# Hybrid decoder trunk: the squares of the features begin 24 bytes into wider tiles and come first in GpSimd's sums of squares; an unread tile of ones is dropped

## The chip, the cores and the metric

One core of a Trainium2 chip runs the whole program in one launch. The metric is the device time of one execution in microseconds (us). The kernel before took 1767.26 us in the median of three runs (1767.1 to 1767.7).

## What is computed

The reference is a decoder trunk of two layers on a float32 input of 512 tokens by 1024 features. Each layer is two half-step feed-forward networks (FFNs) around a mixer, and each of the three begins with an RMS norm of x over its features:

```
def rms_norm(x, g):
    y = xf * lax.rsqrt(jnp.mean(xf * xf, axis=-1, keepdims=True) + EPS)
    return (y * g)

x = x + 0.5 * swiglu(rms_norm(x, ffn1_norm[l]), ...)     # 1024 -> 2816 -> 1024
h = rms_norm(x, mix_norm[l])                              # [a | g | q | k | v] = h @ w_in[l]
x = x + concatenate([conv_out, diff_out]) @ w_out[l]      # causal depthwise conv; differential attention
x = x + 0.5 * swiglu(rms_norm(x, ffn2_norm[l]), ...)
```

The change concerns the sum of `xf * xf` over the features, which the norm needs.

## The kernel before, in words

**Layout.** x lies transposed in SBUF: a tile of 128 partitions (features within a block) by 8 blocks k by 512 tokens, called `x[:, k, :]`. A matrix product is made of float32r products of high and low parts: `hi` is a rounded copy, `lo` the rest, and each block needs three matmuls (hi·hi, hi·lo, lo·hi). Weights arrive by DMA in `wraw` tiles and are split into `whi` (ScalarE, L106 and L370) and `wlo` (VectorE or GpSimd, L107; VectorE, L374).

**The norm's preparation.** Class `Prep` makes, for the next sub-layer, from each block k of x as soon as the previous sub-layer has finished it:
- `acth`: the block times its gain, rounded (ScalarE, L231);
- `actl`: the rest (VectorE, L232, with x and `acth` as tensors from SBUF);
- the squares: ScalarE squares the block into `sq`, a ring of two buffers, or for k = 0 directly into `ssum` (L240), and GpSimd adds `sq` to the running sum `ssum` (L244). The very first sub-layer does these seven sums on VectorE instead.

The first products of the next sub-layer use `acth` and `actl` without the norm's factor. Beside them TensorE transposes `ssum` (L201, `rows_rstd`), VectorE sums over features (L205), and the factor, one number for each token, is spread back (L214, `spread`) and multiplied in behind the products. So the sums of squares are needed by L201, some matmuls after the last block of x is finished. There are five such stages with seven sums on GpSimd each: the end of the first FFN and of the mixer in each layer, and the end of the second FFN of the first layer.

**Other users.** The FFN reuses the two `sq` buffers, and that of `ssum`, for parts `hs` of its hidden features (`Gated.part`), which are moving operands of matmuls at L387. The mixer uses `sq` for squares of queries, keys and outputs (L912, L1067), and the setup for a few small tiles. The mixer's convolution has sums of squares of its own, in a form that matters here (L961 to L963):

```
sq = mt.tile([P, SEQ + 8], F32, tag="csq", name="csq", bufs=1)[:, GAP : GAP + SEQ]
S.activation(sq, y, AF.Square)
G.tensor_tensor(csum, sq, csum, op=ALU.add)
```

`GAP` is 6 elements, 24 bytes. The convolution's taps are summed by GpSimd as well (L982: `yp` begins `GAP` elements into a tile of `SEQ + 8`, and `prod` at a tile's start). So are the sums of weight blocks for the FFN's products (`Unit.sums`, L360 to L363): `g1` and `g2` lie in a tile that begins `GAP` elements in; `u1` and `u2` are, in the units of the down projection, blocks of one tile from its start.

**Addresses.** Tiles of a pool get consecutive places in each partition, in the order in which their tags are first used. The tile `ones` lies in the first pool, behind `ident`, and nothing reads it; in its pool and in those behind it, every tile starts on a multiple of 32 bytes. `ssum` and the two `sq` buffers are neighbours, 2048 bytes each.

**Order.** Each engine runs its instructions in one queue; the order between independent steps is chosen when the program is built, and is fixed then.

Of the kernel before, what the change touches and what calls it, by code (L numbers as in the profile page):

```python
# [11 lines left out]
F32 = mybir.dt.float32  # L12
# [3 lines left out]
ALU = mybir.AluOpType  # L16
AX = mybir.AxisListType

P = 128
DEPTH = 2  # L20
SEQ = 512
# [28 lines left out]
GAP = 6  # L50
# [20 lines left out]
def trunk(ctx: ExitStack, tc: tile.TileContext, xt, par, lamv, relb, onehot,  # L71
          gu1, dn1, wag, wqkv, wout, gu2, dn2, out):
    nc = tc.nc
    V, S, G, T = nc.vector, nc.scalar, nc.gpsimd, nc.tensor

    const = ctx.enter_context(tc.tile_pool(name="const", bufs=1))
# [4 lines left out]
    tmp = ctx.enter_context(tc.tile_pool(name="tmp", bufs=2))  # L81
# [97 lines left out]
    lead = [[tuple(t[1:]) for t in lead[2 * m : 2 * m + 2]] for m in range(2)]  # L179
    ident = const.tile([P, P], F32, tag="ident", name="ident")  # L180
    make_identity(nc, ident)
    ones = const.tile([P, P], F32, tag="ones", name="ones")
    G.memset(ones, 1.0)
    mhalf = const.tile([P, 16], F32, tag="mhalf", name="mhalf")
    G.memset(mhalf, -0.5)

# [34 lines left out]
    class Prep:  # L221
# [14 lines left out]
                self.squares(k)  # L236

        def squares(self, k, pin=False):
            sq = self.s if k == 0 else tmp.tile([P, SEQ], F32, tag="sq", name="sq")
            square = S.activation(sq, x[:, k, :], AF.Square)  # L240
            if pin:
                tc.keep_in_program_order(square)
            if k > 0:
                (V if pin else G).tensor_tensor(self.s, self.s, sq, op=ALU.add)  # L244

        def __getitem__(self, k):
            return self.hi[:, k, :], self.lo[:, k, :]
# [1009 lines left out]
```

## Time and profile before

| | us |
|---|---|
| median of three runs | 1767.26 (1767.1 to 1767.7) |
| the profiled execution | 1767.6 |
| its span, first to last instruction | 1765.8 |
| TensorE busy (PE) | 1756.3 (99%) |
| VectorE busy (DVE) | 1394.2 (79%) |
| ScalarE busy (ACT) | 989.1 (56%) |
| GpSimd busy (POOL) | 869.5 (49%) |
| all sums of squares on GpSimd, L244, 35 of 128x512 | 52.2 |

The granted TensorE clock was 1.000 throughout. PE is matmuls, PEld the weight loads that overlap them. In rows by line and form, what follows the first bar is busy time in us and the mean ns of one instruction, and what follows the second is the idle time of the engine just before these instructions, with what ended it. In rows of one tile or line, three numbers are the shortest, middle and longest duration in ns. In rows of the waits, the numbers are us in total, how often, and the longest. In rows in order of time: start, length in us, engine, line, operation, out<-in. A matmul's end is modelled: the starts of matmuls tell more than their lengths.

### The profile page before, as it was taken

Reading aid. Unit: us, or ns where it says so; the run is one execution under the profiler, and the core shown is the slowest. Engines: PE = TensorE matmul, PEld = TensorE weight load, DVE = VectorE, ACT = ScalarE, POOL = GpSimd, SP = SyncE. Lnnn points to the kernel's source line nnn. Section 1 sums busy time; section 2 is a strip of 40 time slices with the busy share of each in tenths; the row PEclk is TensorE's granted clock in tenths of the full one; section 3 lists DMA queues with packets and bytes.
Section 4 is the critical chain, followed back from the end, with each engine's and each line's share of the span. In section 5 each row is a group of like instructions: output and inputs, shape, how many; then the busy total and the mean of one; then the engine's idle time right before and its main releaser. Section 6 shows DMA issues by size and latency. Waiting matters only on the chain.

```text
span 1765.8 us, 30565 instructions
## 1 busy us (share of the span) xinstructions
PE 1756.3 (99%) x11869; PEld 1620.8 (92%) x11869; DVE 1394.2 (79%) x2021; ACT 989.1 (56%) x1591; POOL 869.5 (49%) x665
## 2 busy tenths in 40 slices
PE   9999999999999999999999999999999999999999
PEld 7899999988788899999988999999887888999998
DVE  6978878868857868878778788777788588788785
ACT  6456565545845456556534665565558354565653
POOL 3165655369753146555303565543687432556551
PEclk9999999999999999999999999999999999999999
DMA  6233333333122233333332333334230232333332
GB/s 226 92 117 100 106 108 105 127 104 99 33 84 84 84 96 108 109 102 117 106 108 72 108 99 105 108 98 154 72 119 25 72 108 72 107 98 108 108 106 75
DMA packets 82930, 177.89 MB, mean 101 GB/s; under 512 B 8951, under 2 KB 30726, under 8 KB 82784
## 3 DMA queue, kind: packets, MB, share of 16 engines
q1 hardware_dynamic: 81184, 174.10, 31.2%
q8 instruction: 93, 1.52, 0.4%
q0 software_dynamic: 1312, 1.67, 0.3%
q14 instruction: 53, 0.43, 0.1%
q10 hardware_dynamic: 288, 0.16, 0.0%
HBM read 173.79 MB, written 3.42 MB: 100 GB/s over the span
## 4 chain that ended last, share of the span: by engine, by line
PE 97%; DVE 2%; DMA 0%; issue 0%; SPq 0%; ACT 0%; DVEq 0%
PE ps_pair L387 57%; PE ps_pair L147 5%; PE ps_pair L146 5%; PE ps_pair L143 5%; PE ps_d L147 2%; PE ps_d L146 2%; PE ps_d L143 2%; PE ps_sc L1028 2%; PE ps_d L387 2%; PE ps_pair L904 2%; PE ps_pair L905 2%; PE ps_pair L906 2%; PE ps_out L146 1%; PE ps_out L147 1%; PE ps_out L143 1%; PE ps_o L1058 1%
## 5 line engine op out<-in xcount | busy, mean ns | idle before, releaser
L374 DVE TENSOR_TENSOR wlo<-wraw,whi 128x1024 fp32r<-128x1024 f32 (+2 forms) x400 | 505.6, 1264 | 167.3 <-ACT whi L370 166.6
L370 ACT ACTIVATE whi<-wraw 128x1024 fp32r<-128x1024 f32 (+2 forms) x400 | 379.2, 949 | 329.4 <-PE ps_pair L387 184.5
L360 POOL TENSOR_TENSOR wraw<-wraw 128x512 f32<-128x512 f32 (+1 forms) x100 | 113.1, 1131 | 605.9 <-DVE wlo L374 393.9
L387 PE MATMUL ps_pair<-acth,wlo 128*128 128x256 f32 x1088 | 307.9, 283 | 0.0
L387 PE MATMUL ps_pair<-actl,whi 128*128 128x256 f32 x1088 | 307.9, 283 | 0.0
L387 PE MATMUL ps_pair<-acth,whi 128*128 128x256 f32 x1088 | 307.9, 283 | 0.0
L387 PE MATMUL ps_pair<-th,whi 128*128 128x256 f32 x816 | 230.9, 283 | 0.0
L387 PE MATMUL ps_pair<-tl,whi 128*128 128x256 f32 x816 | 230.9, 283 | 0.0
L387 PE MATMUL ps_pair<-th,wlo 128*128 128x256 f32 x816 | 230.9, 283 | 0.0
L387 PEld LDWEIGHTS ps_pair<-actl,whi 128*128 128x128 f32 x1088 | 208.9, 192 | 0.2
L387 PEld LDWEIGHTS ps_pair<-acth,whi 128*128 128x128 f32 x1088 | 208.9, 192 | 0.2
L106 ACT ACTIVATE whi<-wraw 128x1024 fp32r<-128x1024 f32 (+3 forms) x124 | 123.2, 1002 | 153.0 <-PE ps_pair L146 85.7
L387 PEld LDWEIGHTS ps_pair<-acth,wlo 128*128 128x128 f32 x1088 | 208.9, 192 | 0.0
L362 POOL TENSOR_TENSOR wraw<-wraw 128x512 f32<-128x512 f32 (+1 forms) x100 | 176.5, 1765 | 7.8
L146 PE MATMUL ps_pair<-actl,whi 128*128 128x512 f32 x448 | 174.7, 391 | 0.3
L143 PE MATMUL ps_pair<-acth,whi 128*128 128x512 f32 x448 | 173.7, 392 | 0.7 <-ACT whi L106 0.6
L147 PE MATMUL ps_pair<-acth,wlo 128*128 128x512 f32 x448 | 173.8, 390 | 0.0
L387 PEld LDWEIGHTS ps_pair<-th,whi 128*128 128x128 f32 x816 | 156.7, 192 | 0.0
L387 PEld LDWEIGHTS ps_pair<-tl,whi 128*128 128x128 f32 x816 | 156.7, 192 | 0.0
L387 PEld LDWEIGHTS ps_pair<-th,wlo 128*128 128x128 f32 x816 | 156.7, 192 | 0.0
L363 POOL TENSOR_TENSOR wraw<-wraw 128x512 f32<-128x512 f32 (+1 forms) x100 | 143.1, 1431 | 7.8
L387 PE MATMUL ps_pair<-hl,whi 128*128 128x256 f32 (+1 forms) x496 | 145.6, 294 | 0.0
(205 smaller groups left out, 4382.5 us busy)
## 6 DMA issues: line engine op xcount, KB each, us to landing
wraw<-in_gu SPq DMA_DIRECT2D x172, 512.0 KB, 3.8
wraw<-in_wqkv SPq DMA_DIRECT2D x24, 512.0 KB, 3.7
wraw<-in_wag SPq DMA_DIRECT2D x16, 512.0 KB, 3.6
wraw<-in_wout SPq DMA_DIRECT2D x16, 512.0 KB, 3.5
wraw<-in_dn SPq DMA_DIRECT2D x60, 128.0 KB, 3.1
wraw<-in_dn SPq DMA_DIRECT2D x20, 384.0 KB, 3.2
wraw<-in_dn SPq DMA_DIRECT2D x28, 256.0 KB, 3.2
wraw<-in_dn SPq DMA_DIRECT2D x20, 320.0 KB, 3.5
```

Source lines behind the costliest of these rows:

```text
L106: S.activation(hi, raw, AF.Copy)
L143: first = T.matmul(ps, wh, xh, start=start, stop=False)
L146: T.matmul(ps, wh, xl, start=False, stop=False)
L147: T.matmul(ps, wl, xh, start=False, stop=stop)
L360: G.tensor_tensor(d, g1, u1, op=ALU.add)
L362: G.tensor_tensor(m0, g1, u1, op=ALU.add)
L363: G.tensor_tensor(m1, g2, m0, op=ALU.add)
L370: pinned(S.activation(hi, raw, AF.Copy), pin)
L374: pinned(V.tensor_tensor(out=lo, in0=raw, in1=f32(hi), op=ALU.subtract), pin)
L387: mm = T.matmul(ps, l, r, start=first and i == n == 0, stop=False, skip_group_check=True)
L904: T.matmul(ps[n], xh[:, t], wh, start=k == 0, stop=False)
L905: T.matmul(ps[n], xh[:, t], wl, start=False, stop=False)
```

## The change

The square's tile gets eight elements more (2080 bytes, not 2048), and its 512 elements begin six elements, 24 bytes, into it. In the sum, the square is the first operand and the running sum the second. The tile `ones` and its memset go. `GAP` and the form `SEQ + 8` are those of the convolution's sums.

```
-    ones = const.tile([P, P], F32, tag="ones", name="ones")
-    G.memset(ones, 1.0)
     mhalf = const.tile([P, 16], F32, tag="mhalf", name="mhalf")
...
         def squares(self, k, pin=False):
-            sq = self.s if k == 0 else tmp.tile([P, SEQ], F32, tag="sq", name="sq")
+            sq = self.s if k == 0 else tmp.tile([P, SEQ + 8], F32, tag="sq", name="sq")[:, GAP : GAP + SEQ]
             square = S.activation(sq, x[:, k, :], AF.Square)
             if pin:
                 tc.keep_in_program_order(square)
             if k > 0:
-                (V if pin else G).tensor_tensor(self.s, self.s, sq, op=ALU.add)
+                (V if pin else G).tensor_tensor(self.s, sq, self.s, op=ALU.add)
```

Line numbers behind the dropped lines are two lower in the changed kernel (L244 is L242 there). The other users of the `sq` ring keep their 512 elements at the start of the wider buffers. In the built programs the tiles from `mhalf` on lie 512 bytes lower, those behind the `sq` ring 448 lower. `ssum` and the first `sq` buffer begin 32 bytes past a multiple of 64, before and after; the second buffer did too, and now begins on a multiple of 64.

The order of instructions is the same on every engine but GpSimd. There it differs at the start of the program, whose rows before are these (`gq` is a small tile of products of gains, one for each layer):

```order
masks.py:197 MEMSET ident 128x128
L183 MEMSET ones 128x128
L185 MEMSET mhalf 128x16
L832 MEMSET gq_540 128x2
masks.py:199 ISA
masks.py:199 AFFINE_SELECT ident<-ident 128x128
L832 MEMSET gq_560 128x2
L798 DMA relb<-in_relb 32x4
```

and after:

```order
masks.py:197 MEMSET ident 128x128
L183 MEMSET mhalf 128x16
L830 MEMSET gq_538 128x2
L830 MEMSET gq_558 128x2
masks.py:199 ISA
masks.py:199 AFFINE_SELECT ident<-ident 128x128
L796 DMA relb<-in_relb 32x4
```

One memset is gone, and the second `gq` memset stands ahead of the identity's select. The other place is where the mixer ends, in the first layer, on GpSimd: the last weight split and the attention's last norm, the seven sums, the norm's power, and the first weight sums of the FFN. Before:

```order
L107 TENSOR_TENSOR wlo<-wraw,whi 128x1024 x5
L1070 TENSOR_TENSOR so<-so,se 128x4
L194 TENSOR_TENSOR rs_y<-so,mhalf 128x4
L107 TENSOR_TENSOR wlo<-wraw,whi 128x1024
L244 TENSOR_TENSOR ssum<-ssum,sq 128x512 x7
L194 TENSOR_TENSOR rs_y<-rowv,mhalf 128x4
L360 TENSOR_TENSOR wraw_6645<-wraw 128x512
```

After:

```order
L107 TENSOR_TENSOR wlo<-wraw,whi 128x1024 x5
L1068 TENSOR_TENSOR so<-so,se 128x4
L192 TENSOR_TENSOR rs_y<-so,mhalf 128x4
L107 TENSOR_TENSOR wlo<-wraw,whi 128x1024
L242 TENSOR_TENSOR ssum<-sq,ssum 128x512 x7
L192 TENSOR_TENSOR rs_y<-rowv,mhalf 128x4
L358 TENSOR_TENSOR wraw_6643<-wraw 128x512
```

Nothing moved here but the operands of the sums.

More of the change, by code (lines that the diff above doesn't have):

```diff
@@ L181, in trunk @@
     make_identity(nc, ident)
-    ones = const.tile([P, P], F32, tag="ones", name="ones")
-    G.memset(ones, 1.0)
     mhalf = const.tile([P, 16], F32, tag="mhalf", name="mhalf")
@@ L238, in squares @@
         def squares(self, k, pin=False):
-            sq = self.s if k == 0 else tmp.tile([P, SEQ], F32, tag="sq", name="sq")
+            sq = self.s if k == 0 else tmp.tile([P, SEQ + 8], F32, tag="sq", name="sq")[:, GAP : GAP + SEQ]
             square = S.activation(sq, x[:, k, :], AF.Square)
@@ L243, in squares @@
             if k > 0:
-                (V if pin else G).tensor_tensor(self.s, self.s, sq, op=ALU.add)
+                (V if pin else G).tensor_tensor(self.s, sq, self.s, op=ALU.add)
         def __getitem__(self, k):
```

## The prediction

> **What bounds the kernel now.** The first view is the top of the page: busy time, then the chain that ended last.
>
> ```profile
> span 1765.8 us, 30565 instructions
> PE 1756.3 (99%) x11869; PEld 1620.8 (92%) x11869; DVE 1394.2 (79%) x2021; ACT 989.1 (56%) x1591; POOL 869.5 (49%) x665
> PE 97%; DVE 2%; DMA 0%; issue 0%; SPq 0%; ACT 0%; DVEq 0%
> ```
>
> TensorE is busy for 1756.3 of 1765.8 us and makes up 97% of the chain; GpSimd (POOL), whose sums are edited, is busy for half the span. So a faster sum matters only where TensorE waits for something that the sum holds up. There are few such places. The second view is the table of waits, for TensorE's weight loads, whose waits show what a matmul stood still for:
>
> ```profile
> PEld ps_o L1058 <- DVE actl L1088: 2.1, 2, 1.1
> PEld ps_pair L146 <- DVE actl L232: 1.8, 5, 0.6
> ```
>
> The first is a wait in attention, with no sum of squares near it. The second has one: line 232 is VectorE's `actl`, made from the same rows of x, at the same time, as the squares. All its waits together are 1.8 us (five times, the longest 0.6), 0.1% of the span. No line names the sums (L244) as what TensorE waits for. The next view, what reads and writes `ssum`, says who does:
>
> ```profile
> L244 POOL TENSOR_TENSOR ssum<-ssum,sq x35: 1288/1377/2067, 321.2 to 1426.9; 128x512 f32<-128x512 f32 x35
> ...
> L201 PE MATMUL ps_rows<-ident,ssum x24: 270/272/273, 30.9 to 1431.6; 128*128 128x128 f32 x24
> L244 DVE TENSOR_TENSOR ssum<-ssum,sq x7: 687/693/693, 18.5 to 24.3; 128x512 f32<-128x512 f32 x7
> ...
>   ACT sq L240: 89.0, 30
> ...
>   ACT sq L240: 1.1, 3
> ```
>
> There are 35 sums on GpSimd, 1288 ns at the least and 1377 in the middle. They themselves sat waiting 89.0 us for ScalarE's squares, and held ScalarE up for 1.1 us in all (three waits for a free `sq` buffer). The transposes that read `ssum` (L201) stand in no row of TensorE's waits.
>
> **What the change does to a sum.** Before, both operands begin at the start of tiles whose distance is a multiple of 32 bytes; after, the square begins 24 bytes later (six elements), and comes first. The trace of before has both kinds on GpSimd, by line and form:
>
> ```profile
> L982 POOL TENSOR_TENSOR yp<-yp,prod 128x512 f32<-128x512 f32 x78 | 85.2, 1093 | 24.5 <-ACT prod L981 22.1
> L963 POOL TENSOR_TENSOR csum<-csq,csum 128x512 f32<-128x512 f32 x6 | 6.6, 1093 | 4.6 <-ACT csq L962 3.0 <-ACT csum L959 1.6
> L244 POOL TENSOR_TENSOR ssum<-ssum,sq 128x512 f32<-128x512 f32 x35 | 52.2, 1492 | 89.2 <-ACT sq L240 88.8
> L361 POOL TENSOR_TENSOR wraw<-wraw 128x384 f32<-128x384 f32 x16 | 16.3, 1019 | 1.0
> L360 POOL TENSOR_TENSOR wraw<-wraw 128x384 f32<-128x384 f32 x16 | 13.9, 866 | 91.1 <-DVE wlo L374 81.0 <-DMA wraw<-in_dn 10.1
> ```
>
> L963 is the same computation in the form that L244 is to get: a square 24 bytes into a wider tile, added first to a sum at a tile's start: 1093 ns. L982 has the offset on the running sum, in place and first, and takes 1093 too, so it isn't the order of the operands that counts. The 384-wide pair settles which quantity it is: L360 adds a tile 24 bytes in to one at its start, L361 adds two blocks of one tile; 866 against 1019 ns, 18% more, and 1288 is 18% over 1093. I take 1093 ns for an undisturbed sum after, **0.195 us less** than the 1288 of the shortest now. Its two `sq` buffers will be 24 and, the ring being 32 bytes wider, 56 bytes off a multiple of 64 from `ssum`; L982 alternates between buffers in just that way. 35 × 0.195 = 6.8 us less on GpSimd, if each keeps its waiting; at most, with all sums at 1093, 35 × (1.492 − 1.093) = 14.0 us.
>
> A rule speaks against this. The Trainium skill's GPSIMD Engine Reference, section 3 (Performance versus the Vector engine), says that GpSimd's two reads take turns at one port, which makes some 2.5 cycles per element a floor of the architecture; addresses have no part in it. At the page's 1.2 GHz that is an estimate of 1.07 us for 512 elements, the class of 1093; taken at its word, the edit would leave every sum as it is, and the time with it (the first rival). Rows L360 and L361 disagree with the rule where it is silent.
>
> **Where a shorter sum reaches TensorE.** The sums stand in five stages: the end of the first FFN, of the mixer, and so on. Busy time by stage:
>
> ```profile
> 320.00:356.00 36.00, 36.00 (x235) 32.91 (x234) 28.62 (x31) 20.80 (x31) 14.01 (x15) 1.00 0.46 151
> 536.00:556.00 20.00, 19.86 (x120) 17.30 (x119) 18.53 (x19) 12.79 (x20) 11.57 (x7) 1.00 0.32 103
> 856.00:900.00 44.00, 44.00 (x271) 39.54 (x270) 29.27 (x32) 21.54 (x32) 13.93 (x11) 1.00 0.34 108
> 1197.00:1233.00 36.00, 36.00 (x236) 32.91 (x234) 27.47 (x31) 20.68 (x31) 14.24 (x15) 1.00 0.46 153
> 1413.00:1433.00 20.00, 19.85 (x119) 17.31 (x118) 18.62 (x19) 12.78 (x20) 11.57 (x7) 1.00 0.34 106
> ```
>
> After the length come TensorE, its loads, VectorE, ScalarE and GpSimd. In the three stages that an FFN ends (21 sums), TensorE has no idle time: the sums are worth nothing there, hidden by the matmuls. In the two that the mixer ends (14 sums), VectorE is the full one, 18.53 of 20 us, and TensorE idles for 0.14 and 0.15 (its matmuls' modelled ends cover part of a stall, so I take the starts below). The stretch behind that, in order of time:
>
> ```profile
> 548.34 1.60 POOL L244 TENSOR_TENSOR ssum<-ssum,sq 128x512 f32<-128x512 f32 x1 [1.62 <-ACT sq L240]
> ...
> 548.72 1.78 DVE L232 SCALAR_TENSOR_TENSOR actl<-x,par,acth 128x512 fp32r<-128x512 f32 x1
> ...
> 550.02 1.62 POOL L244 TENSOR_TENSOR ssum<-ssum,sq 128x512 f32<-128x512 f32 x1
> ...
> 550.42 1.78 DVE L232 SCALAR_TENSOR_TENSOR actl<-x,par,acth 128x512 fp32r<-128x512 f32 x1
> ...
> 553.25 0.74 DVE L232 SCALAR_TENSOR_TENSOR actl<-x,par,acth 128x512 fp32r<-128x512 f32 x1
> 553.28 0.39 PE L147 MATMUL ps_pair<-acth,wlo 128*128 128x512 f32 x1
> ...
> 553.51 0.40 PE L143 MATMUL ps_pair<-acth,whi 128*128 128x512 f32 x1
> 554.05 0.19 PEld L146 LDWEIGHTS ps_pair<-actl,whi 128*128 128x128 f32 x1 [0.58 <-DVE actl L232]
> 554.05 0.50 PE L146 MATMUL ps_pair<-actl,whi 128*128 128x512 f32 x1
> ```
>
> Undisturbed, L232 takes 0.74; beside a sum 1.78, 1.04 more; and a sum there takes 1.60 and 1.62, 0.31 more than 1288. The two engines take turns: VectorE is through 0.55 and 0.56 us after the sum that started ahead of it. The Trainium skill's SBUF — State Buffer, section Who interferes with whom, has it as an exclusive lock (a VectorE instruction with two inputs in SBUF against a GpSimd one that reads SBUF, the loser blocked throughout); the trace agrees (1.78 against 0.74), and by proportional sharing the delay would shrink less.
>
> So each of these two sums, 0.195 us shorter, brings VectorE on by 0.195: the last `actl` ends at 553.60 where it ended at 553.99. Earlier sums of the stage can add to that, up to 7 × 0.195 = 1.4 us, as far as VectorE is not held by TensorE's `ps_out`. TensorE needs this `actl` one beat after 553.51, and its beat is 0.23 (553.28 to 553.51), so at 553.74. The stall is 554.05 − 553.74 = **0.31 us**, and 0.39 covers it. In the second layer:
>
> ```profile
> 1430.16 0.39 PE L147 MATMUL ps_pair<-acth,wlo 128*128 128x512 f32 x1
> 1430.38 0.40 PE L143 MATMUL ps_pair<-acth,whi 128*128 128x512 f32 x1
> 1430.93 0.51 PE L146 MATMUL ps_pair<-actl,whi 128*128 128x512 f32 x1
> ```
>
> 1430.93 − 1430.38 − 0.22 = 0.33. Next behind the stall is TensorE's own stream, which has no further wait there. Together **0.64 us**. Between bounds: nothing if the wait stays, 1.8 us if all that the table of waits puts down to L232 goes.
>
> **The other parts.** The dropped memset is one instruction on GpSimd at the start:
>
> ```profile
> 0.87 0.20 POOL L183 MEMSET ones<- 128x128 f32 x1
> PE ps_idle L167 <- DVE relb L797: 1.0, 1, 1.0
> L962 ACT ACTIVATE csq<-u 128x512 f32<-128x512 f32 x6 | 3.8, 633 | 0.0
> L240 ACT ACTIVATE sq<-x 128x512 f32<-128x512 f32 x42 | 25.8, 618 | 2.8 <-DVE x L1150 1.7 <-DVE ssum L244 1.1
> L1049 PE MATMUL ps_at<-ident,e 128*128 128x128 f32 x80 | 14.1, 274 | 0.0
> L1058 PE MATMUL ps_o<-vv,at 128*128 128x128 f32 x160 | 22.6, 276 | 1.6 <-DVE actl L1088 1.6
> ```
>
> TensorE waits there for VectorE, not GpSimd: nothing, 0.2 us at most. ScalarE writes its 42 squares 24 bytes in: by L962 against L240 15 ns more each, 0.6 us, beside matmuls on an engine that is 56% busy; in a mixer stage 7 × 0.015 = 0.1 us could come off the 0.39, which still covers 0.31. The seven sums on VectorE at the start (687 to 693 ns) keep their engine. No row has them with the offset; if they changed by GpSimd's 18%, either way, it would be 0.12 us each and 0.9 in all, and the last starts at 24.3 where the first transpose of `ssum` starts at 30.9: nothing. Everything behind the dropped tile moves down by 512 bytes, everything behind `sq` by 448, both multiples of 64: no other GpSimd pair of any length changes its relative place. One thing does: the second `sq` buffer, which the FFN's `hs` parts also use, now starts on a multiple of 64 bytes, not 32 past one, for 40 matmuls of the program. `ident` lies that way as the moving operand of L1049, `vv` the other way in L1058: 274 and 276 ns, no difference; nothing.
>
> The sum: the profiled execution took 1767.6 us (span 1765.8 and 1.8 around it); less 0.64 is 1766.96. The median of the three runs is 0.34 under the profiled one, so in medians 1767.26 − 0.64 = **1766.6**. A measurement of this kernel can tell some 0.2% (3.5 us) from no change, so this is no change, whichever way it falls.
>
> **Rivals.** *The edit doesn't quicken the sum*: by the skill's rule above, L244 stays at 1288 and more; time 1767.26. For it is only that the rule has no address in it, against it L963 and L361. 7%. *GpSimd's time comes off the end*: all 6.8 us, 1760.5; it would need TensorE to wait for GpSimd in the three FFN stages, where its idle time is nil; 2%. *The moved buffer slows matmuls*: the 40 float32r matmuls on it run at a beat of 0.12 now, two in 0.23 (347.84 to 348.07):
>
> ```profile
> 347.84 0.40 PE L387 MATMUL ps_pair<-hs,whi 128*128 128x256 f32 x2
> 348.07 0.28 PE L387 MATMUL ps_pair<-hs,wlo 128*128 128x256 f32 x1
> ```
>
> If a moving operand on a multiple of 64 bytes were read at half rate, each would cost one more beat: 40 × 0.12 = 4.8 us, so 1766.6 + 4.8 = 1771.4. It makes the kernel slower by 0.2% from (3.5 + 0.64) / 40 = 0.10 us a matmul on. Against it stand L1049 and L1058 (of another type, float32); 3%. *The turns fall differently*: a shorter sum frees GpSimd earlier, it gets in ahead of an L232 that came first before, and VectorE waits one whole sum more, 1.09 us per lost turn; with 0.39 in hand, a stage that loses one ends 0.4 us later than now, and two stages 0.8: 1768.0; 5%.
>
> **How the numbers follow.** The forecast has 83%, the rivals 7, 2, 3 and 5. The range takes in the first rival and the lost turns above, 1768.0, and below all 1.8 us of waits for L232, 1765.5, with 0.2 for the spread of the runs: 1765.3 to 1768.0. Faster by over 0.2%: the second rival and something unseen, 3%; slower: the third and as much unseen, 4%; within 93%.
>
> **What would show it.** L244's least time at 1088 to 1100 ns, not 1288, and GpSimd's busy time 7 to 14 us lower; L232 beside a sum at about 1.6, not 1.78; the waits of `ps_pair` L146 for `actl` L232 well under 1.8 us; TensorE's idle time in the two mixer stages at nil. The prediction is wrong if the sums are quick and that wait stays, if the matmuls on `hs` grow, or if the time moves by more than 2 us with the waits unchanged.

## The result, and the profile after

| | median us | ratio to before (95%) |
|---|---|---|
| before, 5 runs beside it | 1767.27 (1767.10 to 1768.81) | |
| after, 5 runs | 1759.73 (1758.51 to 1761.20) | 0.9955 (0.9941 to 0.9970) |

The change makes the kernel faster by 0.45%, 7.5 us; the prediction had no change. The profiled execution of after took 1760.34 us, its span is 7.3 us shorter. Of all executions reported here one counts as slow (4460.57 us, of the run with a shared tile), and the ratio of that run leaves it out. First the top of after's page, busy time and the chain:

```profile
span 1758.5 us, 30564 instructions
PE 1748.9 (99%) x11869; PEld 1613.4 (92%) x11869; DVE 1387.2 (79%) x2021; ACT 989.3 (56%) x1591; POOL 867.6 (49%) x664
PE 99%; DVE 1%; DMA 0%; SPq 0%; issue 0%; ACT 0%
```

The 7.3 us have gone from TensorE's *busy* time (1756.3 to 1748.9, with the same 11869 matmuls), hardly from its waits; GpSimd's fell by 1.9 us only. Now what the prediction watched. The waits of TensorE's weight loads in after:

```profile
PEld ps_o L1056 <- DVE actl L1086: 2.1, 2, 1.1
PEld ps_pair L143 <- ACT whi L106: 2.0, 3, 1.0
...
PEld ps_pair L146 <- DVE actl L230: 0.2, 1, 0.2
```

The sums in after, first by tile, then by line beside VectorE's `actl`:

```profile
L242 POOL TENSOR_TENSOR ssum<-sq,ssum x35: 1090/1426/2164, 319.7 to 1420.6; 128x512 f32<-128x512 f32 x35
```

```profile
L242 POOL TENSOR_TENSOR ssum<-sq,ssum 128x512 f32<-128x512 f32 x35 | 48.8, 1393 | 88.2 <-ACT sq L238 87.4
L230 DVE SCALAR_TENSOR_TENSOR actl<-x,par,acth 128x512 fp32r<-128x512 f32 x48 | 47.7, 1012 | 6.2 <-ACT acth L229 6.1
```

The same line of `actl` in before:

```profile
L232 DVE SCALAR_TENSOR_TENSOR actl<-x,par,acth 128x512 fp32r<-128x512 f32 x48 | 52.2, 1106 | 5.7 <-ACT acth L231 5.7
```

The undisturbed sum is at 1090 ns (predicted 1093), the wait for `actl` has gone from 1.8 to 0.2 us, and in the two mixer ends TensorE no longer idles. These are the stretches of the prediction's table, 1.8 and 4.9 us earlier, where the same work stands:

```profile
534.20:554.20 20.00, 20.00 (x122) 17.83 (x121) 17.31 (x19) 13.14 (x20) 11.34 (x7) 1.00 0.34 106
1408.10:1428.10 20.00, 20.00 (x121) 17.82 (x120) 17.44 (x19) 13.14 (x20) 11.36 (x7) 1.00 0.34 107
```

So what was predicted came about. It cannot be the 7.5 us, though. To see where these are, I took for matmul after matmul (both programs have the same ones in the same order) how much earlier it starts in after, counted from the span's start. At the end of the first FFN, in which GpSimd's sums hold up nothing, it is already 1.80 us; at 548 us (before's time) 1.78; behind the first mixer's end 2.25; at the end of the second FFN 4.39; at 1357 us 6.43; then 1.55 us are lost in one place (told at the end); the second mixer's end gives 0.46 again; at the end 7.3. The two mixer ends are 0.93 of it. The rest comes evenly, inside the FFNs, where TensorE never waits. Two stretches of 60 us there, in before and then in after (length, then busy time and count for TensorE, its loads, VectorE, ScalarE, GpSimd):

```profile
645.00:705.00 60.00, 60.00 (x503) 60.00 (x502) 50.84 (x72) 38.86 (x63) 33.01 (x24) 1.00 0.35 106
735.00:795.00 60.00, 60.00 (x503) 60.00 (x502) 46.96 (x60) 33.86 (x51) 30.94 (x24) 1.00 0.34 104
```

```profile
645.00:705.00 60.00, 60.00 (x505) 60.00 (x505) 52.45 (x73) 38.74 (x64) 33.16 (x24) 1.00 0.33 102
735.00:795.00 60.00, 60.00 (x508) 60.00 (x507) 47.42 (x61) 34.41 (x52) 32.83 (x25) 1.00 0.34 108
```

TensorE is full in all four, at the same granted clock of 1.00, and yet gets through 505 and 508 matmuls where it had 503. Matmul by matmul, in order of time; before, nine matmuls of the FFN:

```profile
197.60 0.28 PE L387 MATMUL ps_pair<-hl,whi 128*128 128x256 f32 x1
...
198.56 0.40 PE L387 MATMUL ps_pair<-hs,whi 128*128 128x256 f32 x2
```

and after, the same nine:

```profile
197.24 0.28 PE L385 MATMUL ps_pair<-hl,whi 128*128 128x256 f32 x1
...
198.18 0.40 PE L385 MATMUL ps_pair<-hs,whi 128*128 128x256 f32 x2
```

Eight steps from start to start take 0.96 us before, 0.12 each, and 0.94 after, 0.1175 each. I call this step the **beat**: the mean time between the starts of two matmuls of one width, from the trace, without steps over 140 ns (260 for 512 columns), which hold a stall. For 256 columns it is 120.0 ns in before, within 0.2, whatever the moving operand. In after it is 120.1 on `acth` and `actl`, but 118.2 on `th`, 117.5 on `tl`, 117.8 on `hh`, 117.5 on `hl` and 117.7 on `hs`. Summed over all matmuls, the steps of 256 columns take 1010.9 us where they took 1020.7, those of 512 679.1 for 677.9, those of 128 51.6 for 50.3: −9.8 + 1.2 + 1.3 = −7.3, the span.

**Theories.** What sets `th`, `tl`, `hh`, `hl` and `hs` apart from `acth`? In the built program of before the tiles of all these moving operands and of all weights (`whi`, `wlo`) begin at the same place modulo 2048 bytes of a partition, and matmuls read them at multiples of 512 bytes from there. The wider `sq` ring (two buffers, 32 bytes each) stands between the weights and the FFN's pool, so the FFN's tiles (`th`, `tl`, `hh`, `hl` and most of `hs`) now lie 64 bytes further from the weights; `acth` does not. The theory: *the distance in a partition between a matmul's moving operand and its weights sets TensorE's beat*. The rivals: the quicker sums and the released lock give the time, by a way that the waits don't show; or it is the absolute place of a tile that counts, not the distance; or one of the other parts (`ones`, the operands' order).

### The profile page after: what moved, and what is told of

Same layout as the page of the kernel before. It is cut to its first block, busy times and chain, and to the rows that moved or that the text cites. A ratio compares the mean times of both kernels' runs of the same rounds, so it can differ in the third digit from the quotient of the medians.

```text
span 1758.5 us, 30564 instructions
## 1 busy us (share of the span) xinstructions
PE 1748.9 (99%) x11869; PEld 1613.4 (92%) x11869; DVE 1387.2 (79%) x2021; ACT 989.3 (56%) x1591; POOL 867.6 (49%) x664
## 4 chain that ended last, share of the span: by engine, by line
PE 99%; DVE 1%; DMA 0%; SPq 0%; issue 0%; ACT 0%
PE ps_pair L385 56%; PE ps_pair L143 6%; PE ps_pair L147 6%; PE ps_pair L146 6%; PE ps_d L143 2%; PE ps_d L147 2%; PE ps_d L146 2%; PE ps_sc L1026 2%; PE ps_d L385 2%; PE ps_out L143 2%; PE ps_out L146 2%; PE ps_out L147 2%; PE ps_pair L902 2%; PE ps_pair L903 2%; PE ps_pair L904 2%; PE ps_o L1056 1%
## 5 line engine op out<-in xcount | busy, mean ns | idle before, releaser
L358 POOL TENSOR_TENSOR wraw<-wraw 128x512 f32<-128x512 f32 (+1 forms) x100 | 114.3, 1143 | 597.5 <-DVE wlo L372 385.5
L146 PE MATMUL ps_pair<-actl,whi 128*128 128x512 f32 x448 | 174.5, 390 | 0.0
L385 PE MATMUL ps_pair<-hh,whi 128*128 128x256 f32 (+1 forms) x496 | 144.4, 291 | 0.0
```

The source lines that it names most:

```text
L146: T.matmul(ps, wh, xl, start=False, stop=False)
L358: G.tensor_tensor(d, g1, u1, op=ALU.add)
L385: mm = T.matmul(ps, l, r, start=first and i == n == 0, stop=False, skip_group_check=True)
```

## The experiments

### The layout alone, and the sums alone

**Room only**: before, with nothing but the wider ring; the square stays at the tile's start, the operands in their order, `ones` in its place.

```diff
-            sq = ... tmp.tile([P, SEQ], F32, tag="sq", name="sq")
+            sq = ... tmp.tile([P, SEQ + 8], F32, tag="sq", name="sq")[:, :SEQ]
```

> The squares' buffers are 2080 bytes wide, but the squares stay at their start, the old order of operands and the tile of ones stay: every tile behind the buffers lies 64 bytes higher, and GpSimd's sums are as before. Theory A (the time came from the sums of squares): no change, 1767.3, L244 at 1288 ns at the least. Theory B (the time came from TensorE: the distance of a moving operand from its weights in a partition, 0 before and 64 bytes after, modulo 2048, sets the beat of the 256-wide matmuls): 1759.5 to 1760.5, the beat of the matmuls on th, tl, hh and hl 118 ns where it was 120, L244 still at 1288 at the least.

Measured: 1759.47 us, 0.9954 (0.9942 to 0.9967) of before. Its sums, its wait for `actl`, and the two stretches:

```profile
L244 POOL TENSOR_TENSOR ssum<-ssum,sq x35: 1289/1383/2071, 319.0 to 1420.3; 128x512 f32<-128x512 f32 x35
```

```profile
PEld ps_pair L146 <- DVE actl L232: 1.9, 5, 0.6
```

```profile
645.00:705.00 60.00, 60.00 (x506) 60.00 (x505) 52.45 (x73) 38.78 (x64) 33.35 (x24) 1.00 0.33 101
735.00:795.00 60.00, 60.00 (x507) 60.00 (x506) 47.31 (x62) 34.42 (x52) 32.80 (x25) 1.00 0.35 108
```

Sums and wait are those of before (1289 ns, 1.9 us), the beat and the time are those of after. Theory B had it so.

**Offset only**: all of the change, but the pool with the `sq` ring is opened ahead of the pools with the weights and `acth`, so that everything behind it moves together. Every distance from the weights is as before, but for 144 matmuls on `hs` parts that lie in the buffers of `ssum` and `sq`.

```diff
+    tmp = ctx.enter_context(tc.tile_pool(name="tmp", bufs=2))
     rp = ...
...
-    tmp = ctx.enter_context(tc.tile_pool(name="tmp", bufs=2))
```

> All of the change, but the pool that holds ssum and the squares is opened ahead of those of the weights and of x, so that its width moves weights and moving operands alike: the distance of acth, th, tl, hh and hl from the weights is 0 modulo 2048, as before (only the hs parts in ssum and in the squares' buffers stand otherwise). Theory A: as after, 1759.7. Theory B: the beat on th, tl, hh and hl back at 120 ns, the time at 1766.0 to 1767.3, though L244's least time is 1090; what the sums alone bring is 0 to 0.7 us.

Measured: 1767.99 us, 0.9997 (0.9988 to 1.0006), with before at 1768.06 us beside it.

```profile
L242 POOL TENSOR_TENSOR ssum<-sq,ssum x35: 1092/1422/2173, 320.9 to 1426.3; 128x512 f32<-128x512 f32 x35
```

```profile
PEld ps_pair L146 <- DVE actl L230: 0.2, 1, 0.2
```

```profile
645.00:705.00 60.00, 60.00 (x502) 60.00 (x502) 50.81 (x73) 38.42 (x63) 33.02 (x24) 1.00 0.34 104
735.00:795.00 60.00, 60.00 (x503) 60.00 (x502) 47.95 (x59) 33.14 (x51) 31.06 (x24) 1.00 0.33 102
```

The other way about: sums and wait are those of after, beat and time those of before. The two runs part the change cleanly: the layout is all of its time that the medians show, and what the sums bring is under what they can tell apart. `ones` and the order of the operands are in this kernel too, so they go with the sums.

### Other distances

**`acth` too**: after, with 64 bytes of room behind `acth` and ahead of the weights, so that `acth` and `actl` lie at −64, that is 192 modulo 256, from the weights; the FFN's tiles stay at 64.

```diff
+    act.tile([P, 16], F32, tag="room", name="room")
     pars = []
```

> All of the change, and 64 bytes of unused room behind x, acth and actl: now these lie 64 bytes below a multiple of 2048 from the weights, the FFN's tiles 64 above, as after. Theory A: as after, 1759.7. Theory B, if a distance of 64 either way will do: the 256-wide matmuls on acth and actl (3264 of them) fall from 120 to 118 ns, 6.5 us less, so 1753; if only the moving operand above the weights does, as after.

Measured: 1752.08 us, 0.9910 (0.9897 to 0.9924); the stretches:

```profile
645.00:705.00 60.00, 60.00 (x512) 60.00 (x511) 50.46 (x74) 39.30 (x64) 34.98 (x24) 1.00 0.35 106
735.00:795.00 60.00, 60.00 (x520) 60.00 (x519) 48.79 (x62) 35.93 (x55) 33.97 (x25) 1.00 0.33 106
```

The beat on `acth` fell from 120.0 to 115.1 in the mean, 113 to 114 over long stretches; that on `th` stayed at 118. The operand that was moved is the one that changed. But 512 columns on `acth` rose from 227 to 233. So the time is within 1 us of the 1753 that was expected, but not for the expected reason: the gain on 256 columns is larger than the 2 ns foreseen, and the loss on 512 takes much of it back.

**Distance 256**: before without `ones`, with 256 bytes of room ahead of the FFN's tiles, and nothing else.

```diff
+    tmp.tile([P, 32], F32, tag="room", name="room")
```

> The kernel before without the tile of ones, and with 256 bytes of unused room ahead of ssum: sums as before, the FFN's tiles 256 bytes from a multiple of 2048 from the weights. Theory A: 1767.3. Theory B: if what counts repeats every 128 or 256 bytes, 120 ns a beat and 1767.3; if it repeats at a longer distance, a beat of some 118 and 1759 to 1761.

Measured: 1768.88 us, 1.0002 (0.9993 to 1.0011), a beat of 120.0 on every operand, 502 matmuls in both stretches. At 256 bytes things are as at 0, so the pattern repeats with 256 or a part of it.

**The scan**: before without `ones`, `acth` and the FFN's tiles at other distances, by so much room in the two pools (for 192 it is after with this room).

```diff
+    act.tile([P, A], F32, tag="room", name="room")           # acth at 224, 192, 128, 160: A = 8, 16, 32, 24
+    tmp.tile([P, B], F32, tag="room", name="room", bufs=1)   # FFN at 32, 192, 128, 96: B = 8, 32, 32, 24
```

> The kernel before without the tile of ones, with 32 bytes of unused room between actl and the weights, and 32 between the weights and ssum: acth and actl lie at 224 modulo 256 from the weights (32 below), the FFN's tiles at 32. Theory A (sums): 1767.5. Theory B (distance of the moving operand from its weights): beats of 256-wide matmuls unlike 120 ns in both groups; if 32 bytes do as much as 64, some 118 on th and 115 on acth, and 1752; if what counts is in steps of 64 bytes, 120 and 1767.

> All of the change, 64 bytes of room between actl and the weights, and 128 more between the weights and ssum: acth and actl at 192 modulo 256 as in the run with 64 bytes below, and the FFN's tiles at 192 too (from 64). If the distance counts modulo 256, the 256-wide matmuls on th, tl, hh and hl fall from 118 to 115 ns like those on acth: some 5700 by 3 ns, 17 us less than 1752.1, and the 512-wide on hh rise to 233; so 1736 to 1739. If it counts modulo 128, or if acth has its 115 for another reason, 118 stays and 1752.

> As the run with 32, but with 128 bytes in both places: every FFN and mixer moving operand at 128 modulo 256. If the distance counts modulo 128, all beats are 120 and the time 1767.5; if modulo 256, another beat, below 120, the same in both groups, and less than 1760.

> As the run with 32, but with 96 bytes in both places: acth at 160 modulo 256, the FFN's tiles at 96. Theory A: 1767.5. Theory B: beats between those of the neighbours (64 and 128; 128 and 192), so 113 to 118 ns and 1740 to 1755.

Measured:

| `acth` / FFN at | us | ratio (95%) | beat on `acth` | on `th`, `tl` | 512 columns, `acth` |
|---|---|---|---|---|---|
| 0 / 0 (before) | 1767.9 | | 120.0 | 120.0 | 227 |
| 224 / 32 | 1762.91 | 0.9973 (0.9962 to 0.9984) | 117.5 to 118.7 | 116.7 | 233 |
| 192 / 192 | 1741.92 | 0.9852 (0.9837 to 0.9866) | 113.6 | 113.7 | 233 |
| 128 / 128 | 1774.21 | 1.0038 (1.0023 to 1.0053) | 118.7 | 118.7 | 233 |
| 160 / 96 | 1779.30 | 1.0064 (1.0049 to 1.0079) | 118.0 | 119.4 to 120.4 | 234 |

The time depends on the distance, in both directions. 192 is the best for 256 columns, 0 the best for 512. With 512 columns at 233, beats of 118 to 120 on 256 don't pay, and the kernel is slower than before. 96 and 160 missed what was expected of them altogether; 128 has the beat that was expected (below 120, the same in both groups) but not the time (below 1760); 32 and 224 came out as neither of their two cases. At 192 the first stretch and the waits are:

```profile
645.00:705.00 60.00, 59.91 (x527) 59.61 (x526) 52.32 (x75) 40.82 (x66) 36.14 (x25) 1.00 0.36 111
```

```profile
PEld ps_pair L387 <- DVE hs L701: 2.3, 4, 0.6
...
PEld ps_pair L387 <- ACT keep L442: 1.2, 4, 0.3
```

527 matmuls in 60 us, for 503 in before. It missed the 1736 to 1739 that were expected by 3 us and more. The 512-wide matmuls on `hh`, at 233, had been reckoned with; what had not are two waits, 3.5 us together, that the faster TensorE now meets and before doesn't have.

**Everything higher**: the kernel at 192, with all tiles 32 or 64 bytes further up, weights and moving operands alike (`SPACE`, room in the first pool, 320 or 328 elements for 312).

> The kernel of the run with 192 in both places, with the unread room behind ones_r 32 bytes wider: all that follows lies 32 bytes higher, distances unchanged; moving operands begin at 192 modulo 256, weights at 0, as in the FFN units of the run with two distances. Theory B1 (the distance alone sets the beat): 113 to 114 ns and 1742. Theory B2 (the places themselves modulo 256 count too): beats of 117 to 118 in the FFN, as in that run, and 1765 or more.

> As the last, 64 bytes higher: moving operands at 224 modulo 256, weights at 32. B1: 113 to 114 ns and 1742. B2: something else than 113.6, if only the pair of 160 and 224 has it; 1745 to 1775.

Measured: 1742.41 us, 0.9858 (0.9843 to 0.9873), and 1742.12 us, 0.9854 (0.9839 to 0.9868); unmoved it was 1741.92. The absolute place does nothing here, as it did nothing in offset only; the distance does.

### 0 for 512 columns, 192 for 256: a miss, and what it taught

**Two distances**: `whi` and `wlo` become halves of one tile of 2112 elements, so that a weight block can lie at two places in it: the units of 256 columns find theirs at distance 192, the matmuls of 512 columns at distance 0 (but for 312 of them, at 192; 384 of 256 columns outside the units are at 0).

```diff
+    def both(at=0):
+        t = ring("w")
+        return t[:, at : at + 1024], t[:, at + 1024 : at + 2048]
...
-            hi, lo = ring("whi" + tag, n), ring("wlo" + tag, n)
+            hi, lo = both(16) if not tag else (ring("whi2", 512), ring("wlo2", 512))
```

> All of the change; hi and lo of a weight block share one tile of a ring whose buffers are a multiple of 256 bytes apart, so that the place of the weights in it can be chosen by use: those of 512-wide products at a distance of 0 modulo 256 from every moving operand, those of the 256-wide FFN products 64 bytes further on, so that their moving operands lie at 192. Unused rooms keep all else at 0, and the unread room behind ones_r goes to make space. Theory B: 256-wide FFN matmuls at 113 to 114 ns (8100 by 6 ns, some 50 us less than 120), 512-wide at 227 and not 233 (17 us that the run with 192 lost); together, less some 5 us of new waits as in that run and some more as hi and lo now come free together, 1720 to 1730. Theory A: as after, 1760.

Measured: 1748.94 us, 0.9892 (0.9876 to 0.9909). 512 columns on `acth` took 227 ns, as meant, but 256 columns took 117.8 and not 113.6, in both stretches:

```profile
645.00:705.00 60.00, 60.00 (x512) 60.00 (x511) 53.75 (x74) 39.81 (x64) 31.70 (x24) 1.00 0.34 106
735.00:795.00 60.00, 60.00 (x512) 60.00 (x511) 46.69 (x63) 35.66 (x54) 31.46 (x24) 1.00 0.35 106
```

So distance 192 alone doesn't make 113.6. What else differed? The place of everything (224 bytes lower), `whi` and `wlo` in one tile, the buffers 8448 bytes apart and not 4096. One run for each: two distances with everything 224 bytes higher; 192 with the shared tile, all addresses as at 192; 192 with the `whi` buffers 256 bytes further apart.

```diff
+            return wp.tile([P, 2048], dt, tag=tag, name=tag, bufs=4)     # shared tile, addresses as at 192
...
+        more = 64 if tag == "whi" else 0                                 # buffers further apart
```

> The kernel of the run with two distances, all of it 224 bytes higher: moving operands at 160 modulo 256, the weights of 512-wide products at 160, those of the FFN units at 224, the places of the run with 192. B1: as without the shift, 1749. B2: FFN matmuls at 113 to 114 ns, 512-wide at 227; 7900 by 4 ns less than 1749, and some 5 us of new waits: 1718 to 1728. If hi and lo in one tile were the reason for the 118, it stays at 1749.

> The kernel of the run with 192 in both places, every address of it as there, but hi and lo of a weight block lie in one tile, 4096 bytes apart, in a ring of four such tiles 8192 bytes apart, where before the four hi and the four lo tiles were two rings. B1 as it stands (distance modulo 256 alone): 113 to 114 ns a beat, 1742. If the 4096 bytes between hi and lo are what gave 118 in the run with two distances: 117 to 118 on th and acth, and 1775 or more, since 512-wide matmuls stay at 233. If the buffers 256 bytes off from each other were it: 113 to 114, 1742.

> As the run with 192, but the four hi buffers of the large weights lie 4352 bytes apart, not 4096 (256 more), the lo buffers 4096 as before; all distances modulo 256 stay at 192. B1: 113 to 114 ns and 1742. If buffers that differ by 256 modulo 512 gave 118 in the run with two distances: 117 to 118 in units whose hi and lo differ modulo 512, between 1745 and 1775.

Measured, in this order: 1749.68 us, 0.9899 (0.9882 to 0.9915), beat 118; 1734.91 us, 0.9810 (0.9794 to 0.9827), 113.3 for most of each FFN; 1743.14 us, 0.9858 (0.9841 to 0.9874), 114.3 to 114.7. None of the three is the cause. The shared tile is even a gain, of which the wait for `hs`, 1.1 us there for 2.3, is a part.

The last two take two distances apart: **one distance, padded** is two distances with every block at 192 (`at=16` throughout); **two distances again** has the places of the shared tile, and its 512-wide blocks moved to distance 0.

```diff
-    def both(at=0):
+    def both(at=16):      # one distance, padded; units: both(16)
...
+    def both(at=48):      # two distances again; units: both(0)
```

> The kernel of the run with two distances, but the 512-wide products too take their weights 64 bytes into the shared tile: one distance of 192 modulo 256 throughout, all tiles where they were. If the change of distance between parts of the program gave the 118, the beat of the FFN matmuls falls to 113 to 114 and the 512-wide rise to 233, 1735 to 1742. If it is something in the places of that kernel, 118 stays, the 512-wide rise to 233 and the time to 1765.

> The kernel of the run with 192 and a shared tile (1734.9, its FFN tiles, acth and the FFN's weights where they were modulo 256), the shared tiles 8448 bytes apart, and the 512-wide products with weights 192 bytes further on, at a distance of 0. If the distance sets each matmul's beat by itself: 113 to 114 in the FFN, 227 for the 512-wide, 15 us less than 1734.9: 1720. If the run with two distances showed a rule, 118 and 227: 1749.

Measured: 1740.44 us, 0.9841 (0.9826 to 0.9855), and 1733.85 us, 0.9806 (0.9789 to 0.9822), the fastest of all, but neither the 1720 nor the 1749 that were expected. One distance, padded:

```profile
645.00:705.00 60.00, 60.00 (x532) 60.00 (x531) 52.64 (x77) 41.52 (x66) 34.78 (x24) 1.00 0.34 107
735.00:795.00 60.00, 60.00 (x512) 60.00 (x511) 46.77 (x62) 35.22 (x53) 32.19 (x25) 1.00 0.34 108
```

Two distances again:

```profile
645.00:705.00 60.00, 60.00 (x512) 60.00 (x511) 54.67 (x75) 39.41 (x64) 32.24 (x25) 1.00 0.34 106
735.00:795.00 60.00, 60.00 (x529) 60.00 (x528) 48.78 (x65) 38.08 (x59) 34.26 (x26) 1.00 0.37 114
```

The same program, on the same distance, has 532 matmuls in one stretch and 512 in the other, and the second kernel has them the other way about. There are **two steady beats at distance 192**, 113.3 and 117.8 ns, each held for tens of microseconds and more. Two distances is at 117.8 up to the last fifth of each FFN; its FFNs follow 512-wide matmuls at distance 0, as those of two distances again, which begin at 117.8 too; the kernels whose 512-wide matmuls are at 192 begin at 113.3. A switch in the kernel at 192, in order of time, matmuls first and then their weight loads:

```profile
257.60 0.28 PE L387 MATMUL ps_pair<-tl,whi 128*128 128x256 f32 x1
257.72 0.28 PE L387 MATMUL ps_pair<-th,wlo 128*128 128x256 f32 x1
257.90 0.39 PE L387 MATMUL ps_pair<-th,whi 128*128 128x256 f32 x1
258.12 0.28 PE L387 MATMUL ps_pair<-tl,whi 128*128 128x256 f32 x1
258.24 0.28 PE L387 MATMUL ps_pair<-th,wlo 128*128 128x256 f32 x1
```

```profile
257.61 0.19 PEld L387 LDWEIGHTS ps_pair<-th,wlo 128*128 128x128 f32 x1
257.90 0.19 PEld L387 LDWEIGHTS ps_pair<-th,whi 128*128 128x128 f32 x1
258.01 0.19 PEld L387 LDWEIGHTS ps_pair<-tl,whi 128*128 128x128 f32 x1
```

A weight load starts 0.29 us after the one ahead of it, not 0.11, once; before it the beat is 0.113, behind it 0.118, on the same operands:

```profile
232.00:257.00 25.00, 25.00 (x223) 25.00 (x222) 21.37 (x30) 15.95 (x25) 14.17 (x11) 1.00 0.35 109
262.00:287.00 25.00, 25.00 (x215) 25.00 (x214) 22.31 (x32) 16.23 (x26) 16.14 (x12) 1.00 0.39 123
```

But a late load need not switch the beat. In the same trace, in the second FFN:

```profile
664.69 0.28 PE L387 MATMUL ps_pair<-th,wlo 128*128 128x256 f32 x1
664.87 0.39 PE L387 MATMUL ps_pair<-th,whi 128*128 128x256 f32 x1
665.09 0.28 PE L387 MATMUL ps_pair<-tl,whi 128*128 128x256 f32 x1
```

The steps are 0.18 and 0.22 us here too, and the beat behind them is 113.3 as before them. Of twelve such places on `th` in that trace (a step of 182 to 382 ns in a stretch at 113.3), only the one at 257.72 switched it. So which of the two beats holds depends on what ran before: 512 columns at one distance or the other, and now and then a single late load. The cause of the two beats stays open.

## Why the prediction was wrong

**What bounds the kernel** held: TensorE, 99% in both. From it I drew that only its *waits* could give time. That is the gap: a busy engine can also be busy for less long.

**The sum's duration** held: 1090 ns in after, 1092 in offset only, 1289 with room only. So the first rival, in which the sums stay at 1288 and more, is not borne out. The floor that it went by is not broken either: 2.5 cycles per element, which the Trainium skill's GPSIMD Engine Reference gives in section 2.1 (Instruction dispatch), make an estimate of 1.07 us for 512 elements, and 1090 ns lies above it. Offset and operand order were not run apart; that the offset does it rests on the rows of the prediction. **GpSimd's 7 to 14 us** were mis-sized: L242 gave 3.4 (52.2 to 48.8) and the engine 1.9. The middle duration even rose, from 1377 to 1426 ns. In after's first mixer end, GpSimd's sums in order of time:

```profile
539.49 8.71 POOL L242 TENSOR_TENSOR ssum<-sq,ssum 128x512 f32<-128x512 f32 x5 [0.81 <-ACT sq L238]
```

From the start of the first of these five sums to the end of the last it is 8.71 us; the five themselves take 8.39, 1.68 each, where the same five in before took 8.21. Beside `actl` the shorter sums wait more, and all seven of this stage gave only 0.23 us (11.57 to 11.34). Most of the 3.4 us came off in the three FFN stages, where nothing waits for them.

**The lock and the two stalls** held in mechanism: `actl` fell from 1106 to 1012 ns in the mean, the wait from 1.8 to 0.2 us. The term of 0.64 us measured 0.47 + 0.46 = 0.93: beside the 0.31 that I counted, the next step, from L146 to the transposes at L201, went from 0.33 to 0.23 us. Offset only gains 0.92 us in the same two places; against the median it is lost (0.9997).

**The other parts** is the step that failed: "Everything behind the dropped tile moves down by 512 bytes, everything behind `sq` by 448, both multiples of 64: no other GpSimd pair of any length changes its relative place." It saw that one part of the program moves by 64 bytes against the other, and asked of it only what it does to GpSimd's pairs; for TensorE it looked at 40 matmuls on a single buffer, by their place modulo 64, "nothing". In fact all matmuls on `th`, `tl`, `hh` and `hl` and most of those on `hs`, some 4500 of the 8479 with 256 columns, changed their distance from their weights by 64 bytes. With the rest of `hs`, which lies at 0 or 32 in the buffers of `ssum` and `sq` and goes at 117 to 118 among its neighbours, they are 4800 and take 2.1 ns less each: 10 us, of which 512 columns on `hh` and `hl` take 1.3 back (on `hh`, 227 became 231 and 229). This term was put at zero, with no bound.

**The rivals.** The second (GpSimd's time comes off the end, 1760.5) lies within 0.8 us of the result by chance: room only has the whole gain with GpSimd's sums as in before. The third (the moved buffer slows matmuls) asked the right question, of too few matmuls and with one sign. Turns lost to the lock did not show in TensorE's time; their price had a slip, since 1.09 less the 0.39 in hand is 0.70 us a stage, not 0.4, which would have put that rival and the top of the range at 1768.7. The prediction's own test, that it is wrong "if the time moves by more than 2 us with the waits unchanged", is what happened, near enough: 0.9 us of 7.5 are waits.

The Trainium skill, TensorE: Matmul & The Clock Gate, section Part 2: What happens when you issue a matmul, gives the moving operand and the weight load two independent read ports, so that loading the next weights takes no read bandwidth from the running matmul; where the two operands lie has no part in it. No run here shows the ports. What the runs show is that at the same clock the same matmuls start 113.3 to 120.9 ns apart by the distance of their two operands, and at 192 by what ran before. What in the chip makes it so, they don't show.

## What to carry to other kernels

A tile that gets wider moves every tile behind it: ask of each operand of the *bounding* engine where it now lies against the other operands of the same instruction, not only of the instruction that was edited. When an edit changes layout and work at once, run the layout alone (the same room, nothing in it) and the work alone (the same work, all distances kept) before believing in either. In a kernel that TensorE fills, count matmuls in equal stretches: equal busy time and clock with another count is a gain that no table of waits shows.

## What the runs showed of the hardware

- **TensorE's beat depends on the distance between moving operand and weights in a partition, modulo 256 bytes** (float32r; 0 and 256 alike, other repeats not tried). For 256 columns: 120.0 ns at 0, 116.7 to 117.1 at 32, 117.5 to 118.3 at 64, 118.9 to 120.9 at 96, 118.7 at 128, 118.0 at 160, 113.3 or 117.8 at 192, 117.5 to 118.7 at 224. For 512 columns: 227 at 0, 227 to 231 at 64, 233 to 234 at 32 and from 128 to 224. In this kernel that spans 1733.85 to 1779.30 us, 2.6%. Neighbours can count too: in after, the 232 matmuls on `hs` that stay at 0, among others at 64, go at 118.3 and not at 120.0.
- **At one distance there can be two steady beats**, 113.3 and 117.8 ns at 192, chosen by what ran before.
- **A dip of the granted clock** behind the pause in attention costs 1.55 us in some executions. The 1.55 us that after lost on the way are one. The stretch in before, then the one that begins with the same work in after (the clock is the third number from the end):

```profile
1366.00:1381.00 15.00, 13.41 (x81) 11.31 (x81) 12.50 (x45) 11.54 (x39) 12.14 (x14) 1.00 0.00 0
```

```profile
1360.00:1375.00 15.00, 13.42 (x71) 11.54 (x70) 12.11 (x43) 11.37 (x36) 10.64 (x12) 0.89 0.00 0
```

Offset only has one in its first layer, also at 0.89, room only has none. The five executions of after alone go the same way: 1758.5 and 1758.7 us at a mean clock of 1.000, 1759.7 and 1760.3 at 0.999, 1761.2 at 0.998. So two profiled spans can differ by 1.5 us without the change having a part in it: the place where the lag of the same matmul jumps tells such a dip from the change.
